# Second attention: 32-row rotary products and two full score passes in place of three, query rotary rows by DRAM

## The chip, the core and the metric

The kernel runs on one core of a Trainium2 chip. Five engines work side by side, each through its own instructions in order: TensorE (PE) multiplies matrices and writes to PSUM, VectorE (DVE) and ScalarE (ACT) do element work and read PSUM, GpSimd (POOL) does element work in SBUF, and SyncE (SP) issues DMA transfers. Instructions of different engines wait for each other by semaphores. The metric is the device time of one execution in microseconds (us); less is better.

## What is computed

A trunk of two layers over 1024 positions of width 1024. The first layer mixes positions by dilated window attention, the second by latent attention with 16 heads, which is where the change is. Cut to that mixer:

```python
def rope(x, cos, sin):
    x1, x2 = x[..., :half], x[..., half:]
    return jnp.concatenate([x1 * cos - x2 * sin, x2 * cos + x1 * sin], axis=-1)

def mixer_mla(u, w_in, q_norm, w_uq, kv_norm, w_ukv, w_out):
    cq, ckv, k_rope, gate = jnp.split(u @ w_in, ...)
    q = (rmsnorm(cq, q_norm) @ w_uq).reshape(B, S, 16, 64 + 32)
    q_nope, q_rope = q[..., :64], q[..., 64:]
    kv = (rmsnorm(ckv, kv_norm) @ w_ukv).reshape(B, S, 16, 64 + 64)
    k_nope, v = kv[..., :64], kv[..., 64:]
    q_rope, k_rope = rope(q_rope, ...), rope(k_rope, ...)
    # for each block of 128 queries, all 16 heads:
    s = (q_nope @ k_nope.T + q_rope @ k_rope.T) * 96 ** -0.5
    o = softmax(s) @ v
    return (o * silu(gate)) @ w_out
```

A head's score is a product over 96 rows: 64 of its own (nope) and 32 rotary ones. The rotary key rows are the same for all heads.

## The kernel before, in words

Every float32 operand of a product is split in two parts, high and low (`h` and `l`): high is the value rounded to the matmul's type, low what is left. `mm3` (lines 89 to 94) makes three PE passes of it: high by high, low by high, high by low. The profile names these passes L92, L93 and L94 wherever they stand; they are told apart by the tile they write.

The second attention is `layer_b_attention`. Its work is 128 **units**: 16 heads by 8 blocks of 128 queries, with all 1024 keys at once. One loop emits it with a lag between its parts, and PE and SP keep the order in which the loop writes their instructions; ACT, DVE and POOL are ordered by the scheduler at build time, and in that order they run. For unit u:

- `front(u)`: scores into the PSUM tile `s` (128 queries by 1024 keys, two banks; two such buffers), three passes for each half of the keys.
- `soft(u)`: DVE takes the row maximum of `s`, negated, into `mb` (L1328).
- `expo(u)`: ACT writes the exponential into `pr` and its row sums into `den` (L1336).
- `middle(u)`: two iterations later, eight PE transposes of `pr` into two PSUM tiles `t` (L1368), cast by ACT to `pth` (L1371), the rest split off by DVE to `ptl` (L1372).
- `back(w)`: for two units at once, 16 PE passes of 256 columns that multiply by the values `vq` into the tile `o` (L1388); for every second w a transpose of the denominators (L1391). ACT copies `o` out as `osum` (L1397, L1398; the denominators as `rden`, L1349), POOL adds its halves and multiplies by the gate (L1399, L1400).

The tiles `t`, `o` and the products of the preparation share four PSUM banks.

Preparation runs inside the loop as generators, one step per call of `next`: `b_qk(p)` makes the q and k rows of the two heads of pair p (9 passes for each half of the positions), `b_turn(p)` the rotary rows of the queries of four heads (12 passes, products with the cosine and sine table on DVE, sums on POOL), `b_v` the values of four heads. A tile of q or k (128 rows) holds the 64 nope rows above and, below, 64 rows for the rotary part, 32 of them filled and the others zero, so that two neighbouring heads share the rotary query rows and differ in where the key rows stand. `b_rope_rows` copies the key rows from tile to tile by DMA of POOL's queue (L1219). `latents_t` puts the rotary key rows into the first two `kb` tiles.

## Time and profile before

| what | value |
|---|---|
| median of 3 runs | 1365.49 us (1363.44 to 1368.98) |
| the profiled execution | 1372.24 us |
| its span, first to last instruction | 1370.4 us |
| mean granted TensorE clock | 0.987 |
| first and last score pass of the second attention start at | 791.2 and 1259.3 us |
| DMA, mean of the span | 83 GB/s |

The span goes from the profile's first instruction to its last; the 1.8 us beside it belong to the execution and to no engine. A busy time is the sum of the time in which an engine had an instruction under way. On PE instructions overlap (a pass of 512 columns lasts 0.39 us and the next starts 0.23 us after it), so distances between starts say what a pass costs. In a row of instructions, the bracket at the end gives the idle time of the engine just before it and the instruction that ended it. A group's row gives its count, then busy time, mean duration in ns, and idle time before it.

### The profile page before, as it was taken

The numbers are of one execution on the slowest core, as the hardware profiler recorded it, in microseconds if no ns is written. First come the engines' busy times: TensorE is split into PE (matmuls) and PEld (weight loads), VectorE is DVE, ScalarE is ACT, GpSimd is POOL, SyncE is SP. The second block draws the span as 40 slices with busy tenths as digits, with TensorE's granted clock in tenths as the row PEclk, the third lists the DMA queues.
The fourth block names the chain that finished last, engine by engine and source line by source line (L and its number), as shares of the span: only waits on it lengthen the run. The fifth ranks groups of instructions, "written<-read, shape, count | busy, mean of one in ns | idle before, by whom it ended". The sixth has DMA issues, their size and how long they took to land.

```text
span 1370.4 us, 20504 instructions
## 1 busy us (share of the span) xinstructions
PE 1339.2 (98%) x7464; PEld 1152.6 (84%) x7464; DVE 855.7 (62%) x1473; ACT 798.4 (58%) x1631; POOL 562.5 (41%) x550
## 2 busy tenths in 40 slices
PE   8999999999999999999999999999999999999997
PEld 7788888888888888888988888898889889898776
DVE  5554454445445344566734278887887887777887
ACT  3575555554443432355742288788788878887421
POOL 0142233123222266614632344744553473444761
PEclk6999999999999999999999999999999999999998
DMA  9422221113244254552154011111112111113322
GB/s 361 109 66 37 60 62 40 37 48 99 85 143 152 64 158 136 186 175 115 62 143 153 0 34 30 24 41 25 30 27 54 30 24 28 25 55 118 114 93 92
DMA packets 44980, 114.28 MB, mean 83 GB/s; under 512 B 6917, under 2 KB 13333, under 8 KB 44880
## 3 DMA queue, kind: packets, MB, share of 16 engines
q1 hardware_dynamic: 40184, 100.43, 24.0%
q0 software_dynamic: 4096, 12.24, 3.6%
q8 instruction: 59, 0.97, 0.3%
q14 instruction: 41, 0.34, 0.1%
q10 hardware_dynamic: 600, 0.32, 0.1%
HBM read 96.42 MB, written 8.67 MB: 77 GB/s over the span
## 4 chain that ended last, share of the span: by engine, by line
PE 73%; DVE 10%; ACT 7%; DMA 5%; issue 4%; SPq 0%; POOL 0%; DVEq 0%; ACTq 0%; POOLq 0%
PE pj L92 8%; PE pj L94 8%; PE pj L93 8%; PE o L1388 6%; PE t L1368 5%; PE s L92 3%; PE s L94 3%; PE s L93 3%; DMA ada<-ada_row 3%; PE ip L265 3%; PE po L92 2%; PE po L94 2%; PE po L93 2%; DVE mb L1328 2%; PE t L564 2%
## 5 line engine op out<-in xcount | busy, mean ns | idle before, releaser
L92 PE MATMUL pj<-uh,wh 128*128 128x512 f32 x528 | 217.5, 412 | 0.0
L94 PE MATMUL pj<-uh,wl 128*128 128x512 f32 x528 | 207.5, 393 | 0.0
L93 PE MATMUL pj<-ul,wh 128*128 128x512 f32 x528 | 207.3, 393 | 0.0
L1328 DVE TENSOR_REDUCE mb<-s 128x1 f32<-128x1024 f32 x128 | 155.6, 1216 | 48.8 <-PE s L94 47.9
L1372 DVE TENSOR_TENSOR ptl<-t,pth 128x512 fp32r<-128x512 f32 x256 | 165.0, 680 | 5.3 <-ACT pth L1371 3.2
L1371 ACT CAST pth<-t 128x512 fp32r<-128x512 f32 x256 | 139.4, 589 | 37.8 <-PE t L1368 34.4
L105 POOL TENSOR_TENSOR wl<-wraw,wh 128x1024 fp32r<-128x1024 f32 x42 | 106.2, 2533 | 123.0 <-ACT wh L104 93.2
L1336 ACT ACTIVATE pr<-s,mb 128x1024 f32<-128x1024 f32 x128 | 144.2, 1126 | 15.1 <-DVE mb L1328 14.5
L1368 PEld LDWEIGHTS t<-ident,pr 128*128 128x128 f32 x1024 | 119.3, 141 | 19.0 <-DVE ptl L1372 2.8
L1368 PE MATMUL t<-ident,pr 128*128 128x128 f32 x1024 | 133.0, 272 | 2.1 <-DVE ptl L1372 2.1
L1388 PE MATMUL o<-pth,vq 128*128 128x256 f32 x512 | 130.4, 292 | 1.1 <-DVE ptl L1372 1.1
L1388 PE MATMUL o<-ptl,vq 128*128 128x256 f32 x512 | 125.5, 283 | 2.0 <-DVE ptl L1372 1.8
L553 ACT ACTIVATE sb<-sb,stat 128x256 f32<-128x256 f32 (+1 forms) x144 | 67.0, 466 | 95.2 <-DVE stat L547 95.1
L94 PEld LDWEIGHTS pj<-uh,wl 128*128 128x128 f32 x528 | 99.4, 188 | 22.3
L1399 POOL TENSOR_TENSOR osum<-osum 64x256 f32<-64x256 f32 x64 | 47.7, 746 | 163.5 <-ACT osum L1398 162.3
L93 PEld LDWEIGHTS pj<-ul,wh 128*128 128x128 f32 x528 | 100.1, 190 | 14.0
L92 PEld LDWEIGHTS pj<-uh,wh 128*128 128x128 f32 x528 | 99.9, 189 | 14.2
L92 PE MATMUL s<-kb,q 128*128 128x512 f32 x256 | 105.8, 413 | 0.1
L94 PE MATMUL s<-kb,q 128*128 128x512 f32 x256 | 100.4, 392 | 0.0
L93 PE MATMUL s<-kb,q 128*128 128x512 f32 x256 | 100.4, 392 | 0.0
L1388 PEld LDWEIGHTS o<-ptl,vq 128*128 128x128 f32 x512 | 97.8, 191 | 3.0 <-DVE ptl L1372 3.0
L1388 PEld LDWEIGHTS o<-pth,vq 128*128 128x128 f32 x512 | 97.5, 191 | 1.7 <-DVE ptl L1372 1.6
(289 smaller groups left out, 3151.2 us busy)
## 6 DMA issues: line engine op xcount, KB each, us to landing
wraw<-wa SPq DMA_DIRECT2D x36, 512.0 KB
ada<-ada_row SPq DMA_DIRECT2D x64, 256.0 KB
wraw<-wo_a SPq DMA_DIRECT2D x18, 512.0 KB
ada<-ada_ss SPq DMA_DIRECT2D x16, 512.0 KB
kb<-kb POOLq DMA_DIRECT2D x30, 256.0 KB, 4.6
f<-f_d SPq DMA_DIRECT2D x18, 256.0 KB
xc<-xt SPq DMA_DIRECT2D x8, 512.0 KB
xr<-x SPq DMA_DIRECT2D x8, 512.0 KB
```

The lines of the kernel that those rows point to most:

```text
L92: mm(out, wh, xh, start=start, stop=False)
L93: mm(out, wh, xl, start=False, stop=False)
L94: mm(out, wl, xh, start=False, stop=stop)
L105: (lo_engine or self.nc.gpsimd).tensor_tensor(l[:, :width], raw[:, :width], f32(h[:, :width]), op=ALU.subtract)
L553: nc.scalar.activation(sb[:, a * w : a * w + w], sb[:, a * w : a * w + w], AF.Exp, bias=stat[:, 0, hh, t : t + 1], scale=-1.0, accum_out=s ...
L1328: nc.vector.tensor_reduce(m[:, 0:1], s, axis=AX.X, op=ALU.max, negate=True)
L1336: nc.scalar.activation(pr, s, AF.Exp, bias=m[:, 0:1], accum_out=dens[u // 8][:, u % 8 : u % 8 + 1])
L1368: nc.tensor.transpose(pt[:, c * P : c * P + P], pr[:, kt * P : kt * P + P], self.ident)
L1371: nc.scalar.copy(h, src)
L1372: nc.vector.tensor_tensor(l, src, f32(h), op=ALU.subtract)
L1388: nc.tensor.matmul(po[:, 0:256], v, pts[j][x][:, c * 256 : c * 256 + 256], start=n == 0, stop=n == 15)
L1399: nc.gpsimd.tensor_tensor(w3[mine, 0:256], w3[mine, 256:512], w3[mine, 0:256], op=ALU.add)
```

## The change

The rotary key rows go into one tile `kr`, whose four strips of 32 rows hold high parts of the two halves of the keys, twice. The lower 64 rows of the q and k tiles now hold what the second and third pass needed, so that two full passes cover the nope rows' three terms and the rotary rows' low terms: `qa` with the high nope rows above and their low part below, against `k[0]` with the high key rows twice; `qb` with the high nope rows and the rotary rows, against `k[1]` with the low key rows and the rotary key terms. The remaining term, high rotary by high rotary, is four products of 32 rows (`tile_position` 0, 32, 64 and 96) that serve two units: strips 0 and 1 the two key halves of the first unit, strips 2 and 3 of the second. `front` therefore makes two units at once and claims both `s` buffers, and the loop goes in steps of two units.

The query's rotary rows are added in place on POOL, split on ACT and POOL, written to DRAM by SP and read back by SP into the lower half of `qb` and into the strips of a tile `q3`. For all pairs but the first, the second copy of the q and k rows is made by SP's DMA instead of a second ACT copy. The key rows for all later heads are copied once before the loop.

```diff
@@ layer_b_in @@
+        self.kr = self.M.tile([P, 512], F32R, name="kr")
-        nc.gpsimd.memset(latn, 0.0)
-            for c in (400, 448):
-                nc.vector.tensor_tensor(t[:, c : c + 16], tmp[:, 0:16], tmp[:, 32:48], op=ALU.subtract)
-                nc.vector.tensor_tensor(t[:, c + 32 : c + 48], tmp[:, 16:32], tmp[:, 48:64], op=ALU.add)
+            rot = t[:, 384:512].rearrange("p (g a c) -> p g a c", g=4, a=2)
+            x = [tmp[:, 16 * n : 16 * n + 16].unsqueeze(1).to_broadcast([P, 4, 16]) for n in range(4)]
+            nc.vector.tensor_tensor(rot[:, :, 0, :], x[0], x[2], op=ALU.subtract)
+            nc.vector.tensor_tensor(rot[:, :, 1, :], x[1], x[3], op=ALU.add)
...
-            for e, (h, l) in enumerate(self.kb):
-                dst.append((h[64:128, c : c + P], l[64:128, c : c + P], slice(64 - 64 * e, 128 - 64 * e), 3))
...
+            for rows in ((slice(0, P),) if i < 4 else (slice(32, 64), slice(96, 128))):
+                nc.scalar.copy(self.kr[rows, sl], pt[rows, 3 * P : 4 * P])
+            nc.vector.tensor_tensor(
+                self.kb[0][1][64:96, c : c + P], pt[32:64, 3 * P : 4 * P], f32(self.kr[32:64, sl]), op=ALU.subtract
+            )
@@ b_rope_rows: once, before the loop @@
-        for src, dst in zip(self.kb[(hd - 2) % 3], self.kb[hd % 3]):
-            self.nc.gpsimd.dma_start(dst[64:128, :], src[64:128, :])
+        for j in range(2):
+            dma(first[96:128, j * 512 : j * 512 + 512], self.kr[32 * j : 32 * j + 32, :])
+        for n in (1, 2):
+            dma(self.kb[n][1][64:128, :], first[64:128, :])
@@ b_turn @@
-                nc.gpsimd.tensor_tensor(dst, ab[row : row + 32, 0:512], ab[row : row + 32, 512:1024], op=op)
-            self.rope[p].append(r0)
+            for rows, op in ((slice(0, 64), ALU.subtract), (slice(64, 128), ALU.add)):
+                nc.gpsimd.tensor_tensor(ab[rows, 0:512], ab[rows, 0:512], ab[rows, 512:1024], op=op)
+            hl = self.ht(F32R, "rope")
+            nc.scalar.activation(hl[:, 0:512], ab[:, 0:512], AF.Copy)
+            nc.gpsimd.tensor_tensor(hl[:, 512:1024], ab[:, 0:512], f32(hl[:, 0:512]), op=ALU.subtract)
+            for a in range(2):
+                for x in range(2):
+                    nc.sync.dma_start(rd[:, x, a, :, sl], f32(hl[64 * a : 64 * a + 64, x * 512 : x * 512 + 512]))
@@ b_qk @@
-        def put(dst, sl, src):
...
-        def rope(hf, part):
...
+            nc.sync.dma_start(f32(qb[64:128, :]), rows.rearrange("x a c t -> (x a c) t"))
+            q3 = third[:, e * 512 : e * 512 + 512]
+            for g in range(4):
+                src = rows[0].rearrange("a c (i z t) -> (a c) i z t", z=2, t=P)[:, :, g // 2, :]
+                nc.sync.dma_start(f32(q3[32 * g : 32 * g + 32, :]).rearrange("p (i t) -> p i t", t=P), src)
...
+        def both(dst, twin, sl, src, rows):
+            nc.scalar.copy(dst[0:64, sl], src)
+            if p:
+                nc.sync.dma_start(f32(twin[rows, sl]), f32(dst[0:64, sl]))
+            else:
+                nc.scalar.copy(twin[rows, sl], src)
...
@@ front @@
-            s = self.PB.tile([P, 1024], F32, tag="s", bufs=2, name=self.nm("s"))
-            ts = slice(t * P, t * P + P)
-            for j in range(2):
-                ks = slice(j * 512, j * 512 + 512)
-                self.mm3(s[:, ks], q[0][:, ts], q[1][:, ts], k[0][:, ks], k[1][:, ks], True, True)
+            s = [self.PB.tile([P, 1024], F32, tag="s", bufs=2, name=self.nm("s")) for _ in range(2)]
+            for g in range(4):
+                rows = slice(32 * g, 32 * g + 32)
+                ks = slice((g % 2) * 512, (g % 2) * 512 + 512)
+                mm(
+                    s[g // 2][:, ks], q3[rows, (t // 2) * P : (t // 2) * P + P], self.kr[rows, :],
+                    start=True, stop=False, tile_position=(32 * g, 0),
+                )
+            for a in range(2):
+                ts = slice((t + a) * P, (t + a) * P + P)
+                for n, (q, kk) in enumerate(((qa, k[0]), (qb, k[1]))):
+                    for j in range(2):
+                        ks = slice(j * 512, j * 512 + 512)
+                        mm(s[a][:, ks], q[:, ts], kk[:, ks], start=False, stop=n == 1)
+                st[u + a] = s[a]
@@ the loop @@
-        for u in range(nu + 4):
-            p, r = u // 16, u % 16
-            if u < nu:
-                front(u)
...
+        for u0 in range(0, nu + 4, 2):
+            if u0 < nu:
+                front(u0)
...
+                soft(u0)
+                soft(u0 + 1)
+            for u in (u0, u0 + 1):
...
+                if 0 <= u - 2 < nu:
+                    middle(u - 2)
...
+                if u < nu:
+                    expo(u)
+                if u == u0 and u >= 4:
...
+                    back((u - 4) // 2)
...
```

What that does to the engines' orders, at three places. PE in the middle of the attention, before: the scores of one unit (`s_8101`) follow a value product, then come the transposes of an older unit and the scores of the next (`s_8128`).

```order
L1391 MATMUL o_8074<-ident,den_7782 4x128
L92 MATMUL s_8101<-kb_5416,q_7074 128x512
L93 MATMUL s_8101<-kb_5417,q_7074 128x512
L94 MATMUL s_8101<-kb_5416,q_7075 128x512
L92 MATMUL s_8101<-kb_5416,q_7074 128x512
L93 MATMUL s_8101<-kb_5417,q_7074 128x512
L94 MATMUL s_8101<-kb_5416,q_7075 128x512
L1368 MATMUL t_8110<-ident,pr_8043 128x128 x4
L1368 MATMUL t_8117<-ident,pr_8043 128x128 x4
L92 MATMUL s_8128<-kb_5418,q_7807 128x512
```

And with the change (the line numbers are the changed file's: L1335 the 32-row products, L1344 the full passes, L1392 the transposes, L1412 the value product), where the names `s_8064` and `s_8065` are the two buffers:

```order
L1335 MATMUL s_8064<-kr,q_1045_7076 128x512 x2
L1335 MATMUL s_8065<-kr,q_1045_7076 128x512 x2
L1344 MATMUL s_8064<-kb_5416,q_7084 128x512 x2
L1344 MATMUL s_8064<-kb_5417,q_7085 128x512 x2
L1344 MATMUL s_8065<-kb_5416,q_7084 128x512 x2
L1344 MATMUL s_8065<-kb_5417,q_7085 128x512 x2
L1392 MATMUL t_8086<-ident,pr_8024 128x128 x4
L1392 MATMUL t_8093<-ident,pr_8024 128x128 x4
L1412 MATMUL o_8102<-pth_8006,vq_6745 128x256
```

Both units' scores now stand together; the sixteen value passes and the transposes of the second unit (`t_8129`, `t_8136`) follow, and then the next four 32-row products, into the same two buffers.

ACT at such a place before: casts of transposes (L1371), an exponential (L1336), the two copies of the value product (L1397, L1398), casts, and the next exponential.

```order
L1371 CAST pth_8137<-t_8141 128x4x128
L1371 CAST pth_8139<-t_8148 128x4x128
L1336 ACTIVATE pr_8156,den_8155<-s_8128,mb_8135 128x1024
L1397 COPY osum_8175<-o_8158 64x256
L1398 COPY osum_8175<-o_8158 64x256
L1371 CAST pth_8137<-t_8197 128x4x128
L1371 CAST pth_8139<-t_8204 128x4x128
L1336 ACTIVATE pr_8211,den_8155<-s_8180,mb_8187 128x1024
```

With the change (L1395 casts, L1360 exponentials, L1373, L1421 and L1422 the copies of the value product):

```order
L1395 CAST pth_8082<-t_8086 128x4x128
L1360 ACTIVATE pr_8100,den_7803<-s_8064,mb_8078 128x1024
L1395 CAST pth_8084<-t_8093 128x4x128
L1373 COPY rden_8120<-o_8102 4x128
L1421 COPY osum_8124<-o_8102 64x256
L1422 COPY osum_8124<-o_8102 64x256
L1360 ACTIVATE pr_8143,den_7803<-s_8065,mb_8080 128x1024
L1395 CAST pth_8082<-t_8129 128x4x128
L1395 CAST pth_8084<-t_8136 128x4x128
```

The second unit's exponential (of `s_8065`) stands behind the copies of the value product, as before, and now ahead of the last two casts.

Behind a `b_turn` ACT has, with the change, the copy of the turned rows (L1260) ahead of the second exponential, and POOL makes those rows (L1258) around an addition of `osum` (L1423). ACT:

```order
L1360 ACTIVATE pr_7635,den_7431<-s_7594,mb_7613 128x1024
L1395 CAST pth_7619<-t_7628 128x4x128
L1421 COPY osum_7654<-o_7637 64x256
L1422 COPY osum_7654<-o_7637 64x256
L1395 CAST pth_7617<-t_7668 128x4x128
L1395 CAST pth_7619<-t_7675 128x4x128
L1260 ACTIVATE rope_7661<-ab_7608 128x512
L1360 ACTIVATE pr_7682,den_7431<-s_7595,mb_7615 128x1024
```

POOL:

```order
L1261 TENSOR_TENSOR rope_7580<-ab_7573,rope_7580 128x512
L1258 TENSOR_TENSOR ab_7608<-ab_7608 64x512
L1423 TENSOR_TENSOR osum_7654<-osum_7654 64x256
L1258 TENSOR_TENSOR ab_7608<-ab_7608 64x512
L1424 TENSOR_TENSOR gT_6151<-osum_7654,gT_6151 64x256
L1261 TENSOR_TENSOR rope_7661<-ab_7608,rope_7661 128x512
```

Before, ACT read the turned rows only in `b_qk`, pairs of units later.

138 lines of the change are left out of this document (62 added, 76 removed).

## The prediction

> **What bounds the kernel now.** I read the page's busy shares first, then the table of stages, the waits of the stage that changes, and its instructions in order of time on three engines.
>
> ```profile
> PE 1339.2 (98%) x7464; PEld 1152.6 (84%) x7464; DVE 855.7 (62%) x1473; ACT 798.4 (58%) x1631; POOL 562.5 (41%) x550
> ```
>
> ```profile
> 900.00:950.00 50.00, 49.54 (x338) 44.67 (x337) 38.00 (x53) 42.76 (x86) 21.34 (x25) 1.00 0.18 39
> ```
>
> ```profile
> PE m L92 <- DVE kb L1298: 3.2, 7, 0.5
> PE t L1368 <- DVE ptl L1372: 2.1, 3, 0.7
> PE o L1388 <- DVE ptl L1372: 1.1, 2, 0.6
> ```
>
> PE is busy 98% of the span. The second line is one stretch of the second attention (busy time of PE, weight loads, DVE, ACT, POOL): PE 49.54 of 50 us, and ACT already 42.76. The last three are all that PE waited for from 800 to 1270 us: 6.4 us. The attention is bound by the number of PE passes, but ACT stands close behind.
>
> ```profile
> L92 PE MATMUL s<-kb,q x256: 389/395/504, 791.2 to 1258.9; 128*128 128x512 f32 x128
> ```
>
> So the stage is the 468 us from the first score pass to the last. Two consecutive pairs of units on PE:
>
> ```profile
> 899.56 0.48 PE L92 MATMUL s<-kb,q 128*128 128x512 f32 x1
> ...
> 901.82 0.36 PE L1388 MATMUL o<-pth,vq 128*128 128x256 f32 x1
> ...
> 903.83 0.48 PE L92 MATMUL s<-kb,q 128*128 128x512 f32 x1
> 904.15 0.40 PE L93 MATMUL s<-kb,q 128*128 128x512 f32 x1
> 904.38 0.39 PE L94 MATMUL s<-kb,q 128*128 128x512 f32 x1
> ...
> 905.31 1.03 PE L1368 MATMUL t<-ident,pr 128*128 128x128 f32 x8
> 906.10 0.48 PE L92 MATMUL s<-kb,q 128*128 128x512 f32 x1
> ...
> 908.35 0.36 PE L1388 MATMUL o<-pth,vq 128*128 128x256 f32 x1
> ...
> 910.34 0.40 PE L92 MATMUL s<-kb,q 128*128 128x512 f32 x1
> ...
> 912.52 0.48 PE L92 MATMUL s<-kb,q 128*128 128x512 f32 x1
> ```
>
> Durations overlap, so I use distances between starts. A score pass costs 0.23 us (904.15 to 904.38), the first of a run 0.32. Six take 1.48 (903.83 to 905.31), eight transposes 0.79 (905.31 to 906.10), the value product 1.99 (908.35 to 910.34). A pair of units costs (912.52 - 899.56)/2 = **6.48 us**, with no gap.
>
> **The change part by part.** *Removed passes.* Twelve score passes of a pair become eight plus a group of four 32-row products. Eight take 1.48 + 2 x 0.23 = 1.94. No row shows 32-row products. If the four run together the group costs one pass, 0.23; if one after the other, 0.92. I take 0.45: one pass, plus twice the 0.09 by which a first pass exceeds the others, rounded up. PE's work in a pair is then 0.45 + 1.94 + 2 x 0.79 + 1.99 = 5.96, against 6.48: 0.52 less, 33 us over 64 pairs, if PE stays the bound.
>
> A rule of the Trainium skill (TensorEngine Tiling (Array Packing), Key Properties) speaks against it: a change of the tiling mode drains the array. The rows would price a drain at a pass's duration less its spacing, 0.39 - 0.23 = 0.16, and two a pair make 0.32, so that the group costs 0.55 and 64 pairs lose 6 us of the 33; no run so far shows it.
>
> *The new wait.* Before, the two `s` buffers alternate: a unit's scores wait only for the exponential of two units ago. Now both are claimed at once, and the third 32-row product cannot start until the previous pair's second exponential has read its buffer. Behind it on PE stand all eight passes. ACT works in order and has that exponential behind the two copies of the value product (the order above), which wait for PE. So it is a loop. On ACT and DVE:
>
> ```profile
> 904.11 0.26 ACT L1349 COPY rden<-o 4x128 f32<-4x128 f32 x1 [0.27 <-PE o L1391]
> 904.39 0.36 ACT L1397 COPY osum<-o 64x256 f32<-64x256 f32 x1
> 904.77 0.37 ACT L1398 COPY osum<-o 64x256 f32<-64x256 f32 x1
> 905.94 1.08 ACT L1371 CAST pth<-t 128x512 fp32r<-128x512 f32 x2 [0.81 <-PE t L1368]
> 906.90 1.13 ACT L1336 ACTIVATE pr<-s,mb 128x1024 f32<-128x1024 f32 x1
> 907.91 0.21 ACT L1336 ACTIVATION_READ_ACCUMULATOR pr<-s,mb 128x1 f32 x1
> 908.20 1.07 ACT L1371 CAST pth<-t 128x512 fp32r<-128x512 f32 x2
> ...
> 910.54 0.36 ACT L1397 COPY osum<-o 64x256 f32<-64x256 f32 x1 [0.17 <-PE o L1388]
> ```
>
> ```profile
> 905.51 1.23 DVE L1328 TENSOR_REDUCE mb<-s 128x1 f32<-128x1024 f32 x1 [1.79 <-PE s L94]
> 906.65 1.28 DVE L1372 TENSOR_TENSOR ptl<-t,pth 128x512 fp32r<-128x512 f32 x2
> ```
>
> From the end of one second exponential to the end of the next: hand-over and the two released products 0.45 (bounds 0.23 and 0.92), eight passes 1.94, transposes 0.79, from the value product's start to its first copy 2.19 (908.35 to 910.54), or 2.57 in every second pair with its denominators (901.82 to 904.39), mean 2.38, two copies 0.76, exponential 1.13. The sum is **7.45 us**, longer than PE's 5.96 and longer than the 6.48 of today. Nothing else is later: the first cast comes 0.63 after the transposes start (905.31 to 905.94), at 3.02; the first exponential 0.48 later at 3.5, the second cast 1.30 later (906.90 to 908.20) at 4.8, done in time for the copy at 5.37 at the earliest. DVE must first finish the two splits of the previous transposes: the casts start 0.16 after the loop's start (1.30 less 1.13) and follow 0.48 apart, each split needs 0.6 behind its cast, so the first maximum starts near 2.0; two maxima at 1.14 end by 4.4.
>
> By the order of the change 29 pairs are plain: 29 x (7.45 - 6.48) = **+28**.
>
> *Pairs with preparation products behind the value product* (14 with nine passes, 3 with twelve, 3 with 24 half passes). PE's work there is at least 5.96 + 9 x 0.23 = 8.0, above the loop, so they gain the 0.52: 20 x 0.5 = **-10**.
>
> *Pairs right behind these.* ACT's casts of the new q and k rows stand ahead of its exponentials.
>
> ```profile
> L1270 ACT CAST q<-m 64x512 fp32r<-64x512 f32 x28 | 16.3, 582 | 5.4 <-DVE q L1271 5.2
> L1244 DVE TENSOR_TENSOR ab<-m,cs 64x512 f32<-64x512 f32 x12 | 8.2, 687 | 5.7 <-PE m L94 3.7 <-issue 1.8
> L1279 POOL TENSOR_TENSOR q<-rope,q 64x512 fp32r<-64x512 f32 x16 | 20.3, 1291 | 3.1 <-ACT q L1277 2.8
> L1399 POOL TENSOR_TENSOR osum<-osum 64x256 f32<-64x256 f32 x63 | 46.7, 741 | 163.4 <-ACT osum L1398 162.3
> ```
>
> Behind a `b_qk` or a `b_v` four casts of 0.58, two of 0.48 and a weight split (taken as one more of 0.58) come before or beside the first exponential: 3.9 less the 0.5 that ran ahead, then 1.30, two casts 0.96, two copies 0.76 and 1.13 make 7.6: 10 pairs x 1.1 = **+11**. Behind a `b_turn` the second exponential stands behind a copy that waits for POOL: maxima until 4.6, four DVE products of 0.69 until 7.4, POOL's subtraction 1.29, an `osum` addition 0.74, POOL's addition 1.29, the copy 0.6 and the exponential 1.13 end at 12.4, 5.9 more than now: 3 x 6 = **+18** (bounds 0, if POOL is early, and 18).
>
> *The last pair of heads* has ACT splits of the output weights in four pairs of units, two with the next casts too, ahead of the second exponential:
>
> ```profile
> L104 ACT ACTIVATE wh<-woraw 128x1024 fp32r<-128x1024 f32 x6 | 6.4, 1064 | 1.1 <-DMA woraw<-wo_b 1.1
> ```
>
> 4 x 1.06 and 2 x 0.96: **+6**. Against all this, the stage of today holds some waits of its own: 64 x 6.48 = 415, 162 preparation passes at 0.23 = 37 and 96 half passes at 0.12 (1.99 / 16) = 12 make 464, less 5 for the first pairs, which lack transposes and value product. The 468 hold some 9 more, about half of it first passes of a run at 0.09 and half waits, which the periods above replace: **-5**.
>
> *At nothing:* the rotary rows by DRAM, and the q and k copies now sent by SP. They are issued some 20 us before the head that reads them; the nearest row:
>
> ```profile
> kb<-kb POOLq DMA_DIRECT2D x26, 256.0 KB, 4.6
> ```
>
> 4.6 us to landing. Without that cover each of seven changes of heads would pay up to 4.6, 32 us. On SP only the denominator's two small transfers queue behind them, and those are read five units later. The first pair alone has no such lead: its rows are written and read back while 10 us of gate passes remain: **+2**. The fewer key copies before the attention lie beside a full PE: 0. Fewer ACT casts and POOL subtractions in `b_qk` are in the periods above.
>
> Sum: 28 - 10 + 11 + 18 + 6 - 5 + 2 = **+50 us**. The profiled execution took 1372.2 (span 1370.4 and 1.8 around it), so 1422; it lay 6.7 above the median of 1365.5, where I forecast **1415**.
>
> **The rivals.** *PE stays the bound (the other side).* The 0.52 of every pair is kept: 1365.5 - 33 = **1332**. It decides at 5.96: the second exponential would have to end by then instead of at 7.45. It would, just, if it stood ahead of the copies: first exponential at 3.5, the next 1.30 later, 4.8 + 1.13 = 5.9. ACT's 42.76 busy us in 50 speak for a tight but possible fit; the built order speaks against, in every pair. The Trainium skill (TensorE: Matmul & The Clock Gate, Part 3) gives 3.07 times for four such products; by it the group takes 0.92/3.07 = 0.30, an estimate, and this rival 1322. 5%.
>
> *Only the loop bites.* POOL and the casts are on time and the last pair is no worse: 28 - 10 + 2 = +20, **1386**. For it: preparation overlaps well today. 20%.
>
> *The four products don't run together.* The change then doesn't do what it says: the group costs 0.92, the 20 preparation pairs gain 0.05 and not 0.5, and the loop grows by up to 0.47 in 42 pairs: +50 + 9 + 20 = **1444**. Nothing in this trace speaks for or against. 15%.
>
> **How the numbers follow.** The forecast itself has 57%. The remaining 3% are small offsetting errors that end within 0.5% (about 7 us, what a measurement of this kernel can tell from no change). The range takes in the loop alone at its low end and the serial case at the other: 1384 to 1445, which leaves out the 8% of the other cases. Faster 0.05, same 0.03, slower 0.92.
>
> **What would show it.** PE's share of a plain stretch falls from 99% to about 80%, and a wait of the 32-row products for ACT's exponential, which is absent now, totals 60 to 90 us in some 40 occasions; ACT's copy of `osum` still starts right behind PE. The group shows in four starts within 0.1 us of each other or 0.23 apart. Behind a `b_turn` ACT waits for POOL three times. I am wrong if the distance between groups is near 6 us in plain pairs, or if PE waits for DMA instead.

## The result, and the profile after

| | before | after |
|---|---|---|
| median of 4 runs | 1365.55 us (1363.44 to 1368.98) | **1454.91 us** (1447.96 to 1455.41) |
| ratio, with its 95% interval | | **1.0645** (1.0617 to 1.0673) |
| the profiled execution's span | 1370.4 us | 1453.0 us |
| mean granted TensorE clock | 0.987 | 0.977 |

The change costs 89 us. The forecast was 1415 with a range up to 1445: the direction was right, the size was not. The page of the changed kernel gives the busy time and share of each engine first:

```profile
PE 1361.3 (94%) x7464; PEld 1138.8 (78%) x7464; DVE 863.6 (59%) x1449; ACT 783.6 (54%) x1611; POOL 491.7 (34%) x483
```

The same stretch of the second attention as before (length; busy time and instructions of PE, weight loads, DVE, ACT, POOL; clock; DMA):

```profile
900.00:950.00 50.00, 45.54 (x303) 37.86 (x302) 35.45 (x48) 36.42 (x75) 13.49 (x16) 1.00 0.25 63
```

PE is busy 45.5 of 50 us where it was 49.5, though the change was to save it work. ACT and DVE have become idler too: 36.4 for 42.8 and 35.5 for 38.0. Every engine is idler and the time is longer, which points to engines that wait for each other in a ring. The waits of PE from 790 to 1345 us (engine, line and product, releaser; sum, times, longest):

```profile
PE s L1335 <- ACT pr L1360: 45.8, 43, 2.6
PE t L1392 <- ACT osum L1422: 7.8, 4, 2.4
PE s L1335 <- DMA q<-rope_d: 6.7, 1, 6.7
PE o L1412 <- DVE kb L1314: 5.6, 6, 0.9
PE m L92 <- DVE vq L1221: 3.7, 3, 1.2
```

The first line is the wait that the prediction named. The other four are new as well, and the prediction had none of them as a wait of PE; the third is a wait for DMA, which it had named as a sign of being wrong. A plain pair on PE and ACT, in order of time (start, length, engine, line, operation; idle time before it and what ended it):

```profile
862.99 0.49 PE L1335 MATMUL s<-kr,q 32*128 32x512 f32 x2
...
864.52 0.49 PE L1335 MATMUL s<-kr,q 32*128 32x512 f32 x2 [1.04 <-ACT pr L1360]
864.94 2.12 PE L1344 MATMUL s<-kb,q 128*128 128x512 f32 x8
...
866.90 1.03 PE L1392 MATMUL t<-ident,pr 128*128 128x128 f32 x8
...
870.64 0.49 PE L1335 MATMUL s<-kr,q 32*128 32x512 f32 x2
...
871.96 0.49 PE L1335 MATMUL s<-kr,q 32*128 32x512 f32 x2 [0.82 <-ACT pr L1360]
872.38 2.11 PE L1344 MATMUL s<-kb,q 128*128 128x512 f32 x8
```

```profile
863.26 1.11 ACT L1360 ACTIVATE pr<-s,mb 128x1024 f32<-128x1024 f32 x1
...
869.93 0.36 ACT L1421 COPY osum<-o 64x256 f32<-64x256 f32 x1 [0.23 <-PE o L1412]
870.31 0.37 ACT L1422 COPY osum<-o 64x256 f32<-64x256 f32 x1
870.70 1.11 ACT L1360 ACTIVATE pr<-s,mb 128x1024 f32<-128x1024 f32 x1
```

The ring can be walked through. The second exponential ends at 863.26 + 1.11 = 864.37, the second two 32-row products start at 864.52, the full passes at 864.94, the transposes at 866.90, the copy of the value product on ACT at 869.93, the next second exponential at 870.70, and it ends at 871.81: 7.44 us a turn. This turn has no denominators; the prediction's 7.45 is a mean of turns with and without them, and its sum without them is 7.26. The first two 32-row products (862.99, 870.64) are early and help nothing, since the full passes stand behind the other two. They also hide a part of the wait: it goes from 862.99 to 864.52, 1.53 us, but the profile counts only the 1.04 behind their own 0.49 as idle.

**Where the 82.6 us of the two spans are.** One fixed point lets the parts be compared: the activation that ends the sixth block of gate products, shortly before the rotary rows of the first heads are made.

```profile
762.81 0.60 ACT L1120 ACTIVATE gT<-pg 128x512 f32<-128x512 f32 x1 [4.84 <-PE pg L94]
...
791.17 0.39 PE L92 MATMUL s<-kb,q 128*128 128x512 f32 x1
```

```profile
759.99 0.60 ACT L1127 ACTIVATE gT<-pg 128x512 f32<-128x512 f32 x1 [4.84 <-PE pg L94]
...
787.11 0.47 PE L92 MATMUL m<-lath,wuh 128*128 128x512 f32 x1 [2.37 <-DVE kb L1314]
...
798.18 2.07 PE L1335 MATMUL s<-kr,q 32*128 32x512 f32 x4 [6.73 <-DMA q<-rope_d]
```

The first fence is before, the second after. On SP the trip through DRAM of the same rows looks like this, eight writes and then the first read:

```profile
778.58 8.07 SPq L1264 DMA_DIRECT2D rope_d<-rope  x8
794.48 0.50 SPq L1281 DMA_DIRECT2D q<-rope_d  x1
```

Up to that point the changed kernel was 2.8 ahead; from there to the first full pass (800.19) it takes 40.2 us where 28.4 stood: **+11.8**. The 63 distances between the first full passes of neighbouring pairs of units (before the change: between the first score passes) add up to 536.8 where they were 462.6: **+74.1**. The rest of the span is 0.6 shorter. So the part behind the fixed point went from 607.6 to 693.0, +85.4. By kinds of pairs (mean distance, and what the kind adds in all; the predicted terms by the same kinds):

| pairs | before | after | adds | predicted |
|---|---|---|---|---|
| 18 plain | 6.50 | 7.61 | +20.0 | +17.5 |
| 14 with nine preparation passes, 3 with `b_turn` | 8.92, 9.37 | 8.31, 9.02 | -9.6 | -8.5 |
| 3 with `b_v` | 9.61 | 10.61 | +3.0 | -1.5 |
| 7 behind `b_qk`, 3 behind `b_v` | 6.35, 6.36 | 8.57, 7.32 | +18.4 | +11 |
| 3 behind `b_turn` | 7.37 | 12.21 | +14.5 | +18 |
| 3 behind those | 6.93 | 9.51 | +7.7 | +2.9 |
| 6 of the last heads | 6.76 | 8.89 | +12.8 | +11.8 |
| first 3 | 5.61 | 8.03 | +7.2 | +1.9 |

The predicted column spreads the +28 of the 29 plain pairs over the plain ones (18), those behind the ones behind `b_turn` (3), the last heads (6) and the first (2). It leaves out the prediction's -5 for stalls of before, and the start's +2 against 11.8. With these the prediction had +50 behind the fixed point.

### The profile page after: what moved, and what is told of

Read it like the earlier page. It is cut to its first block, busy times and chain, and to the rows that moved or that the text cites. A ratio compares the mean times of both kernels' runs of the same rounds, so it can differ in the third digit from the quotient of the medians.

```text
span 1453.0 us, 20632 instructions
## 1 busy us (share of the span) xinstructions
PE 1361.3 (94%) x7464; PEld 1138.8 (78%) x7464; DVE 863.6 (59%) x1449; ACT 783.6 (54%) x1611; POOL 491.7 (34%) x483
## 5 line engine op out<-in xcount | busy, mean ns | idle before, releaser
L1395 ACT CAST pth<-t 128x512 fp32r<-128x512 f32 x256 | 140.6, 587 | 96.5 <-PE t L1392 96.2
L1352 DVE TENSOR_REDUCE mb<-s 128x1 f32<-128x1024 f32 x128 | 152.6, 1220 | 30.2 <-PE s L1344 29.4
L1360 ACT ACTIVATE pr<-s,mb 128x1024 f32<-128x1024 f32 x128 | 142.8, 1115 | 35.5 <-DVE mb L1352 34.7
L1344 PE MATMUL s<-kb,q 128*128 128x512 f32 x512 | 144.7, 427 | 0.0
L1392 PE MATMUL t<-ident,pr 128*128 128x128 f32 x1024 | 136.8, 277 | 7.9 <-ACT osum L1422 7.8
L1423 POOL TENSOR_TENSOR osum<-osum 64x256 f32<-64x256 f32 x64 | 47.3, 739 | 279.5 <-ACT osum L1422 276.4
L1392 PEld LDWEIGHTS t<-ident,pr 128*128 128x128 f32 x1024 | 120.0, 143 | 22.4 <-ACT osum L1422 10.1
L1412 PE MATMUL o<-pth,vq 128*128 128x256 f32 x512 | 130.5, 293 | 6.3 <-DVE kb L1314 5.6
L1412 PE MATMUL o<-ptl,vq 128*128 128x256 f32 x512 | 125.1, 282 | 0.0
L1344 PEld LDWEIGHTS s<-kb,q 128*128 128x128 f32 x512 | 97.3, 200 | 34.9 <-issue 16.3
L1335 PE MATMUL s<-kr,q 32*128 32x512 f32 x256 | 56.3, 508 | 52.6 <-ACT pr L1360 45.8
L1412 PEld LDWEIGHTS o<-pth,vq 128*128 128x128 f32 x512 | 97.8, 191 | 8.0 <-ACT pr L1360 6.8
L1412 PEld LDWEIGHTS o<-ptl,vq 128*128 128x128 f32 x512 | 98.0, 191 | 0.0
```

The lines of the kernel that those rows point to most:

```text
L1344: mm(s[a][:, ks], q[:, ts], kk[:, ks], start=False, stop=n == 1)
L1352: nc.vector.tensor_reduce(m[:, 0:1], s, axis=AX.X, op=ALU.max, negate=True)
L1360: nc.scalar.activation(pr, s, AF.Exp, bias=m[:, 0:1], accum_out=dens[u // 8][:, u % 8 : u % 8 + 1])
L1392: nc.tensor.transpose(pt[:, c * P : c * P + P], pr[:, kt * P : kt * P + P], self.ident)
L1395: nc.scalar.copy(h, src)
L1412: nc.tensor.matmul(po[:, 0:256], v, pts[j][x][:, c * 256 : c * 256 + 256], start=n == 0, stop=n == 15)
```

## The experiments

Each edit is made to the changed kernel. "The part behind the fixed point" is the span less the start of that activation, 693.0 in the changed kernel; it is given because the changed kernel and all these edits are the same up to there, and yet their profiled executions reach it at times from 753.7 to 762.7 us. Differences of a few us between medians can come from there.

### Both exponentials ahead of the copies

```diff
+                if u == u0 and u < nu:
+                    expo(u0)
+                    expo(u0 + 1)
-                if u < nu:
-                    expo(u)
                 if u == u0 and u >= 4:
```

> The changed kernel (1454.9 us) with one thing moved: both exponentials of a pair of units are written ahead of the value product, so that on ACT the second one stands ahead of the copies of the value product. Theory 1 (a loop through ACT: second exponential, 32-row products, eight passes, value product, its copies, second exponential): the loop loses the value product and the two copies and becomes hand-over 0.57, passes 1.94, first cast at +0.63 and 0.48 long, exponential with its sum 1.29, cast 0.48, exponential 1.13: 6.5 us in a plain pair where it is 7.44 and 7.77 now. 29 plain pairs give back 30 us, the three pairs behind a b_turn 5 us each, the pairs behind a b_qk some: 1400 to 1420 in all. Rival (the 32-row products and the switch of the array's tiling are what costs): nothing of that is moved here, plain pairs stay at 7.4 to 7.8 and the time at 1450 to 1456.

Measured: **1394.26 us** (1392.67 to 1397.40), ratio 1.0207 (1.0176 to 1.0238); behind the fixed point 635.6, 57.4 less. PE's waits from 790 to 1285 us:

```profile
PE o L1412 <- DVE kb L1314: 5.5, 6, 0.9
PE t L1392 <- DVE ptl L1396: 5.3, 6, 1.3
PE s L1335 <- DMA q<-rope_d: 5.1, 1, 5.1
PE s L1335 <- ACT pr L1360: 3.1, 3, 1.5
```

The 45.8 us of waits for the exponential have shrunk to 3.1, with two lines of the loop moved and no work taken away. Plain pairs fall from 7.61 to 6.51 in the mean. The ring through the copies is shown to be the main cause, and it is worth somewhat more than expected. But 6.51 is just the 6.50 of before: what PE's passes save in a pair does not come back even here.

### One unit's scores first

Two 32-row products and four full passes for the first unit, then the same for the second.

```diff
-            for g in range(4):
-                mm(s[g // 2][:, ks], ..., tile_position=(32 * g, 0))
             for a in range(2):
+                for g in (2 * a, 2 * a + 1):
+                    mm(s[a][:, ks], ..., tile_position=(32 * g, 0))
                 ts = slice((t + a) * P, (t + a) * P + P)
```

> The changed kernel with the four 32-row products in two groups: two of them and the four full passes of the first unit, then two and the four passes of the second, so that the first unit's passes no longer stand behind the wait for the second buffer. Theory 1 (the loop): four passes of 0.23 leave the loop; plain pairs go from 7.6 to about 6.7, 29 of them give back 26 us; the 20 pairs with preparation, bound by PE, pay one more start of a group, about 0.5 each, 10 us: 1432 to 1445. Rival (the switch of the tiling is what costs): twice the switches, at 0.3 to 0.5 us each in 64 pairs, 1475 to 1485.

Measured: **1415.53 us** (1414.89 to 1416.91), ratio 1.0361 (1.0332 to 1.0390); behind the fixed point 658.1. This is the other way to cut the same ring: four full passes no longer stand behind the second exponential. It takes away 34.9 us where at most 23 were expected, with plain pairs at 6.75 to 6.88 and those behind a `b_qk` at 7.4 to 7.6. The mode of the array is changed twice as often here, and the time falls, against the rival's 1475 to 1485.

### DVE's half split left out, alone and with the exponentials ahead

```diff
+                if j == 0:
-                nc.vector.tensor_tensor(l, src, f32(h), op=ALU.subtract)
+                    nc.vector.tensor_tensor(l, src, f32(h), op=ALU.subtract)
...
-                        nc.tensor.matmul(po[:, 0:256], v, pts[j][x][:, ...
+                        nc.tensor.matmul(po[:, 0:256], v, pts[j][x * (1 - j)][:, ...
```

> The change with DVE's split left out for the second half of the keys and nothing else. Theory 1 (the loop of the change runs over PE, ACT's copies and ACT's exponential, and DVE is no part of it): plain pairs stay at 7.4 to 7.8 and the total at 1450 to 1456. Rival (DVE's work is part of what sets the pairs already): plain pairs fall by 0.3 or more, total below 1445.

> Both exponentials ahead of the copies, and DVE's split left out for the second half of the keys (the value product uses the high part twice there, so PE has the same passes): 1.3 us less of DVE in a pair. Theory 1 (with the exponential ahead, plain pairs stand at 6.4 to 6.65 instead of PE's own 6.05 because DVE's two maxima and four splits run one behind the other): plain pairs fall to 6.05 to 6.25, total 1378 to 1386. Rival (ACT's casts, exponentials and copies set them): plain pairs stay within 0.1, total 1391 to 1397.

Measured, alone: **1454.47 us** (1453.14 to 1456.48), ratio 1.0643 (1.0620 to 1.0666), plain pairs 7.4 to 7.8 as without the edit. Taking 1.3 us of splits from DVE in every pair changes nothing, so they are no part of the change's ring. With the exponentials ahead: **1387.19** (1386.53 to 1389.35), ratio 1.0154 (1.0128 to 1.0180), between the two expectations. Pairs of 6.65 and 6.63 fall to 6.28 and 6.35, those of 6.39 stay at 6.45. So DVE's order is part of what keeps the plain pairs above PE's own work. How much PE's own work is, this kernel shows: the first pair here has no wait, and in the second the third and fourth 32-row products come late.

```profile
909.43 2.12 PE L1344 MATMUL s<-kb,q 128*128 128x512 f32 x8
...
915.28 0.50 PE L1335 MATMUL s<-kr,q 32*128 32x512 f32 x4
915.71 2.12 PE L1344 MATMUL s<-kb,q 128*128 128x512 f32 x8
...
921.41 0.81 PE L1335 MATMUL s<-kr,q 32*128 32x512 f32 x4
922.15 2.12 PE L1344 MATMUL s<-kb,q 128*128 128x512 f32 x8
```

915.71 - 909.43 = 6.28 with denominators; without them the pairs behind a `b_v`, which have no wait, take 6.14. So PE's own pair is 6.14 and not the predicted 5.96. Before, the same pairs took 6.54 and 6.37, so the change saves PE 0.2 to 0.3 us in a pair and not 0.52. The second distance is 6.44, because the four products take 0.81 where they take 0.50: a wait of 0.31 for the second buffer that the profile does not count as idle. The waits for the exponential that it does count, 8.3 us now for 3.1, lie outside the plain pairs.

### The group twice

The same loop over the four 32-row products is written a second time, with `start=False`.

> The four 32-row products are issued twice in a row, so the rotary term is counted twice. Theory 1 (the four run together; most of the group's 0.53 us is the change of array mode): the second group costs one pass, 0.23 us, or at most the whole 0.43 again; it lies on the loop or on PE in all 64 pairs, so +15 to +27 us on 1454.9: 1470 to 1482. Rival (the four run one after the other, and 0.53 is only what the trace happens to show): 0.92 us in 64 pairs, +59: about 1514.

Measured: **1469.20 us** (1466.89 to 1471.79), ratio 1.0732 (1.0714 to 1.0751), just under the 1470 to 1482 of theory 1. A plain pair on PE, where L1342 is the second group:

```profile
937.95 0.50 PE L1335 MATMUL s<-kr,q 32*128 32x512 f32 x2 [1.05 <-ACT pr L1367]
937.96 0.73 PE L1342 MATMUL s<-kr,q 32*128 32x512 f32 x4
938.62 2.11 PE L1351 MATMUL s<-kb,q 128*128 128x512 f32 x8
```

Plain pairs become 7.67 where they were 7.44: **0.23 us** for four more products, which is one pass. The four run together, and the rival of 1444 by serial products is out. In the changed kernel, where nothing waits, the group costs this:

```profile
919.49 0.40 PE L94 MATMUL m<-lath,wul 128*128 128x512 f32 x1
...
919.82 0.50 PE L1335 MATMUL s<-kr,q 32*128 32x512 f32 x4
...
920.25 2.10 PE L1344 MATMUL s<-kb,q 128*128 128x512 f32 x8
```

From the last product ahead of it to the first full pass it is 0.76, less that product's own 0.23: 0.53. Less the four products' 0.23, some 0.30 are left for going into the 32-row mode and out of it; behind transposes it is some 0.07 more. The Trainium skill (TensorEngine Tiling (Array Packing), Key Properties) states a drain at a change of mode without a price. These rows would be its price, but they don't show the drain itself; the 0.55 that the prediction worked out for it and did not take is close.

### The turned rows put off

ACT's copy of the turned rotary rows, POOL's split and their DRAM writes come two steps (for the second half four) behind the end of `b_turn`.

```diff
-            hl = self.ht(F32R, "rope")
-            nc.scalar.activation(hl[:, 0:512], ab[:, 0:512], AF.Copy)
...
+            late.append((sl, ab))
+        for sl, ab in late:
+            yield 0.0
+            yield 0.0
+            finish(sl, ab)
```

> The changed kernel with the ACT copy, POOL split and DRAM writes of the turned rotary rows put off by about one pair of units, for all heads but the first four. Theory 2 (the pair behind a b_turn is 12.2 us long because the second exponential stands behind a copy that waits for POOL, and the pair behind that one is 9.1 to 9.95 us long because PE stood idle so long that its clock was halved): the first goes to 8 or 9, the second to 7.5, three times, and the granted clock has no halved stretch there: 1454.9 - 3 x (4 + 2) = 1437, 1432 to 1442. Rival (these pairs are long for PSUM banks held by the products of b_turn): the long pair stays near 12 and the time within 3 us of 1455.

Measured: **1452.69 us** (1450.79 to 1457.26), ratio 1.0635 (1.0593 to 1.0677); behind the fixed point 692.8 against 693.0. The pair behind `b_turn` falls from 12.26 to 9.88, but the next two, 9.95 and 8.25, become 9.75 and 9.83: four pairs together take 37.9 for 38.9 there, and 37.9 for 38.3 and 37.8 for 37.9 at the other two places. The wait of the transposes for ACT's copy turned into one for DVE's split (7.1 us in 3 times). So neither side is right: the long pair did fall, as theory 2 said, but the time moved to the next pairs, and the total is the rival's.

### Idle time filled

Dummy products in the places where PE stands still behind `b_turn`, into parts of PSUM that are overwritten or unused.

```diff
+            if w in (8, 24, 40):
+                for _ in range(40):
+                    nc.tensor.matmul(po[:, 384:512], v, pts[1][1][:, 0:P], start=True, stop=True)
...
+            if u in (22, 54, 86):
+                for _ in range(12):
+                    mm(s[0][:, 0:512], qa[:, 0:P], k[0][:, 0:512], start=True, stop=True)
```

> The changed kernel with products added in the three pairs behind a b_turn only: 40 of 128 columns into an unused part of the value product's bank, and 12 score passes into the first score buffer ahead of the next pair, where they are overwritten. They fill most of the time in which PE waits there. Theory of the clock: PE's idle time is what halves the granted clock for 7 to 10 us; filled, the halved stretches at these three places go, the pair that follows falls from 9.1 to 9.95 to about 7.5, and the time falls by 3 to 8 us in spite of the added work: 1447 to 1452. Rival (the following pair is long for another reason, such as DVE behind its schedule): it stays above 9, and the added passes make the time equal or longer, 1455 to 1462.

The rows that led to it, in the changed kernel behind a `b_turn`, and the clock in the stretches around them (second to last numbers: clock, DMA share, GB/s):

```profile
888.67 1.97 PE L1392 MATMUL t<-ident,pr 128*128 128x128 f32 x8 [2.38 <-ACT osum L1422]
...
892.94 0.80 PE L1335 MATMUL s<-kr,q 32*128 32x512 f32 x2 [1.58 <-ACT pr L1360]
893.66 3.78 PE L1344 MATMUL s<-kb,q 128*128 128x512 f32 x8
```

```profile
885.00:890.00 5.00, 2.62 (x17) 2.42 (x17) 4.45 (x7) 3.11 (x7) 4.10 (x5) 0.84 0.13 34
890.00:895.00 5.00, 3.42 (x11) 1.95 (x10) 1.38 (x2) 2.62 (x5) 2.95 (x3) 0.50 0.25 79
895.00:900.00 5.00, 5.00 (x25) 4.31 (x25) 3.49 (x4) 2.38 (x4) 0.00 (x0) 0.64 0.25 65
```

Behind an idle time of 2.38 us the clock stands at one half for about 10 us, and eight full passes last 3.78 instead of 2.12. With the idle time filled, the clock is full from 813.1 to 1260.2 us (this execution is some 6 us earlier, so the stretches hold slightly later work):

```profile
885.00:890.00 5.00, 5.00 (x26) 3.71 (x25) 1.67 (x3) 2.77 (x6) 2.69 (x3) 1.00 0.26 82
890.00:895.00 5.00, 4.69 (x38) 4.06 (x36) 3.26 (x4) 3.70 (x8) 0.47 (x1) 1.00 0.25 82
```

The pairs behind fall from 9.95, 9.53 and 9.06 to 7.65, 7.66 and 7.66: 5.6 us, of the +7.7 in that row of the table. The filled pairs ahead of them are 1.1 longer each, 3.4 in all, which gives the other engines more time too; but the eight full passes alone, at 3.78, 3.78 and 3.52 instead of 2.12, are 4.7 of the 5.6. So most of that row is the clock. The median is **1447.12** (1445.73 to 1448.96), ratio 1.0592 (1.0561 to 1.0622), inside the expectation; but behind the fixed point it is 692.4 for 693.0, and the profiled execution reached that point 6.2 earlier. The median's gain is therefore no evidence; the pairs and the clock are.

### The first heads' rotary rows earlier

Four kernels: `b_turn(0)`, which makes these rows, made whole ahead of the last gate products; the same with the exponentials ahead and the turned rows put off; `b_turn(0)` two blocks of gate products earlier; and that with the exponentials ahead. The first one's edit:

```diff
-        weave((chain(gate(6, 1, ...), gate(7, 1, ...)), 10368.0), (chain(self.b_turn(0), self.b_qk(0)), 9000.0))
+        for _ in self.b_turn(0):
+            pass
+        weave((chain(gate(6, 1, ...), gate(7, 1, ...)), 10368.0), (self.b_qk(0), 9000.0))
```

> The rotary query rows of the first four heads are made wholly ahead of the last gate products instead of between them, so that their trip through DRAM starts about 2 us earlier on PE's side, and 15 more gate passes (3.4 us) stand between it and the first score pass. Theory 1 (PE's wait of 6.7 us before the first scores is the trip through DRAM): the wait falls to 2 to 4 us, the first full pass starts at 794 to 797 instead of 800.2, and the total falls by 3 to 6: 1449 to 1452. Rival (ACT's and DVE's casts of the first q and k rows are nearly as late): the first full pass at 799 or later, total within 2 us of 1455.

> Three edits together: both exponentials ahead of the copies (1394 alone), the turned rows' copy, split and DRAM writes put off for all but the first four heads, and the first four heads' rows made ahead of the gate products. Theory 1 (with PE near its own bound the put-off rows find room, and the start gains by itself): pairs behind b_turn fall from 8.4 to 9.0 to about 7.5, start -3 to -5: 1384 to 1389. Rival (as when put off alone, the time only moves to the next pairs): pairs 11 and 12 together stay near 16 us, and only the start gains: 1389 to 1393. Neither reaches 1366, because plain pairs stay at 6.4 to 6.6 behind DVE's maxima and splits.

> The rotary query rows of the first four heads are made two blocks of gate products earlier than in the change (some 78 gate passes, 18 us, before the last product they need), so that neither their sums on POOL nor their trip through DRAM is late. From the first product of the preparation to the first full pass the change takes 28.8 us where 17.0 stood before; the passes alone are 17.1. Theory 1 (the waits of 2.4 and 6.7 us and the halved clock behind them are the whole difference): PE waits less than 2 us in all there, and the total falls by 8 to 11: 1444 to 1447. Rival (the casts of the first q and k rows on ACT and DVE are late by themselves): PE still waits 4 us or more for DVE's key split, total 1450 to 1455.

> Both exponentials ahead of the copies (1394.3 alone) and the first four heads' rotary rows two blocks of gate products earlier. If the two losses are separate, the gains add: 1383 to 1387. Rival (the loop hides a late start, since the first pairs then wait for less): 1390 to 1394. Either way above 1367, since the pairs behind the preparation and the plain ones keep their times.

The first: **1455.23** (1449.00 to 1458.75), ratio 1.0625 (1.0595 to 1.0654). PE's wait for the DMA is gone, and PE waits for DVE instead; the first full pass comes 1.4 earlier behind the fixed point, and the first three pairs take 2.3 more:

```profile
789.16 0.77 PE L92 MATMUL m<-lath,wuh 128*128 128x512 f32 x1 [5.32 <-DVE kb L1316]
...
794.86 0.48 PE L92 MATMUL pg<-u1h,wgh 128*128 128x512 f32 x1 [1.66 <-DVE kb L1316]
```

ACT's casts of the first k rows, which that split needs, stand behind ACT's copy of the turned rows, which waits for POOL's sums. The second: **1399.61** (1396.69 to 1404.63), ratio 1.0222 (1.0189 to 1.0254), 4.7 longer behind the fixed point than with the exponentials ahead alone: neither theory, since the pairs behind `b_turn` did not become shorter, those with preparation behind the put-off work became longer (8.22 to 8.62 or 9.24, 9.27 to 9.74 twice), and the start gained only 0.6. The third: **1445.33** (1441.52 to 1453.95), ratio 1.0584 (1.0539 to 1.0629), where 1444 to 1447 was expected; but only 7.0 of it lie behind the fixed point (0.8 ahead of the first full pass, 3.3 in the first three pairs, which ran at full clock, the rest later), and PE still waits, now ahead of other gate products for their weights, with half the clock from 764.3 to 774.6:

```profile
766.40 0.79 PE L92 MATMUL pg<-u1h,wgh 128*128 128x512 f32 x1 [4.56 <-ACT wgh L1170]
...
769.11 0.80 PE L94 MATMUL pg<-u1h,wgl 128*128 128x512 f32 x1 [1.49 <-POOL wgl L1171]
```

The fourth: **1394.75** (1392.15 to 1395.74), ratio 1.0202 (1.0179 to 1.0225), no gain over the exponentials ahead, nearest the rival. So the trip through DRAM is what ends last at the start, but ACT's copy and POOL's sums of the turned rows are nearly as late, and moving them moves the wait. A version without the loss of the start was not found.

### The splits of q, k and v from SBUF

First the key rows alone, then all three; the low parts become zero.

```diff
-                nc.vector.tensor_tensor(k[1][0:64, sl], ps[...], f32(k[0][0:64, sl]), op=ALU.subtract)
+                src = ps[64 * e : 64 * e + 64, :] if p < 2 else f32(k[0][0:64, sl])
+                nc.vector.tensor_tensor(k[1][0:64, sl], src, f32(k[0][0:64, sl]), op=ALU.subtract)
```

> For pairs of heads 2 to 7, DVE's split of the key rows reads the rounded rows in SBUF instead of the product in PSUM (the low part becomes zero), so the product's PSUM bank comes free at ACT's copy; the instruction stays. Theory 1 (the value product waits for that bank): the six pairs behind such a b_qk fall from 8.6 to about 7.7 us, and PE's wait of the value product for DVE's key split goes: 1455 - 6 = about 1449. Rival (the casts of q and k on ACT ahead of the exponentials set those pairs, as predicted with 7.6 but longer): they stay at 8.4 to 8.7, total within 3 us of 1455.

> For pairs of heads 2 to 7 and the values of heads 4 to 15, DVE's splits of the new q, k and value rows read the rounded rows in SBUF (the low parts become zero), so every PSUM bank of a preparation product comes free at ACT's copy. The splits stay as instructions. Theory 1 (banks held until DVE's splits lengthen the pairs behind b_qk and the pairs with b_v): pairs behind b_qk of pairs 2 to 7 fall from 8.57 to about 7.7, the pairs with b_v from 10.6 to about 9.4: 6 x 0.9 + 3 x 1.2 = 9 less, about 1446. Rival (ACT's casts ahead of the exponentials set both kinds): they stay within 0.2, total 1452 to 1457.

> The same with both exponentials ahead of the copies (1394.3 alone). Theory 1 (banks): behind b_qk 7.53 falls to about 6.7, with b_v 10.5 to 9.4, total about 1386. Rival (casts on ACT): within 0.2 of the pairs before, total 1391 to 1397.

The row behind a `b_qk` that led to it, in the changed kernel: the value product waits for a bank of PSUM, not for its data.

```profile
924.16 0.36 PE L1412 MATMUL o<-pth,vq 128*128 128x256 f32 x1 [0.94 <-DVE kb L1314]
```

With the key rows alone: **1458.02** (1454.52 to 1469.28), ratio 1.0664 (1.0618 to 1.0711). That wait fell to 1.0 in all, and a new one took its place, of the transposes for the query rows' split: 7.0 in 5 times. The six pairs did not fall as theory 1 said; they took 7.9 to 9.9, and DVE's key splits themselves became longer (rows below). So this kernel does not tell the two theories apart. With all three: **1446.69** (1442.02 to 1447.71), ratio 1.0578 (1.0549 to 1.0607), behind the fixed point 683.9, 9.1 less. Five of the six pairs concerned fall from 8.6 to 7.4 or 7.5, the sixth from 8.26 to 8.01, and the pairs with `b_v` from 10.61 to 9.89, while two of the three behind these rose from 7.3 to 7.8. The same pair in that kernel, from its first full pass to the next one's:

```profile
920.70 2.12 PE L1344 MATMUL s<-kb,q 128*128 128x512 f32 x8
...
928.16 2.12 PE L1344 MATMUL s<-kb,q 128*128 128x512 f32 x8
```

928.16 - 920.70 = 7.46, a plain turn of the ring. A faster DVE is not the reason. These are its key splits from 860 to 1290 us in the changed kernel, with the key rows alone, and with all three (mean ns is the second number behind the bar):

```profile
L1314 DVE TENSOR_TENSOR kb<-m,kb 64x512 fp32r<-64x512 f32 x24 | 16.5, 686 | 0.4
L1314 DVE TENSOR_TENSOR kb<-kb 64x512 fp32r<-64x512 f32 x24 | 22.4, 955 | 0.3
L1314 DVE TENSOR_TENSOR kb<-kb 64x512 fp32r<-64x512 f32 x24 | 19.0, 802 | 0.2
```

Reading SBUF, the splits last as long or longer (the queries' 683 for 689, the values' 873 for 686). The scheduler orders ACT's and DVE's work here a little differently too, but the time is that of the bank: in the changed kernel the value product starts 3.91 behind the first full pass, right after DVE's key splits end at 924.02, and with all three it starts 2.75 behind it, before those splits begin at 923.71. That is 1.16 of the 1.18 by which this pair falls. So the banks that DVE's splits hold cost these pairs what ACT's casts were predicted to cost. With the exponentials ahead it brings nothing: **1399.52** (1396.80 to 1402.95), ratio 1.0238 (1.0204 to 1.0272), above both expectations. The pairs behind `b_qk` stay at 7.6 to 7.9, and PE waits 15.9 us for DVE's `ptl` splits there. Which order of DVE would serve both was not tried.

## Why the prediction was wrong in size

Of the part behind the fixed point the prediction had +50, and it was +85.4. The mechanism that it named, the ring through the copies, is the largest part of the loss. The 35 us that are missing lie for the most part in three steps of its sum, which stand below under "Wrong". The median missed the forecast by 40 us; what is beyond these 35 lies ahead of the fixed point and in the scatter of the runs.

Right, or nearly so:

- *The new wait.* The ring is as described, and moving the exponentials ahead of the copies takes 57.4 us away. The plain pairs are 7.61 in the mean against 7.45, +2.5 in 18 pairs. The step that was too short is the hand-over, 0.57 from the exponential's end to the full passes instead of 0.45. PE's idle time for it, 45.8 us in 43 times, is less than the 60 to 90 named, and PE's share of the stretch shown fell to 91% and not to 80%. Both miss for one reason: the first two products of a group run during the wait. With their 0.49 in each of 43 times it would be 67 us, an estimate from the rows above.
- *Pairs with preparation*: -0.6 in those with nine passes, against -0.5.
- *Behind a* `b_turn`: 12.2 us against 12.4, by the chain that was worked out. In the first such pair DVE's four products end at 888.21, POOL's two sums with the `osum` addition between them at 891.01, ACT's copy at 891.79 and the second exponential at 892.80.
- *The last pair of heads*: +12.8 against 11.8, in part by luck. The weight splits stand ahead of the second exponential as described, but the clock is at one half from 1301.4 to 1304.8 and from 1311.6 to 1315.0, and eight full passes take 3.33 and 3.56 there instead of 2.11, 2.7 us that the sum didn't have.
- *Own stalls of before: -5.* This is no miss of its own: the table's rows before hold such stalls (7.37 and 6.93 behind `b_turn`, against 6.48).

Wrong, in the order of size:

- *At nothing ... the first pair alone has no such lead: +2.* It was **+11.8** up to the first full pass, and the first three pairs added 7.2 where 1.9 were predicted. The working had the 4.6 us of another transfer as its only price of the trip, and set it against the gate passes that were left. But SP sends its last write at 785.82 and can send the first read only at 794.48, when the writes have landed: 8.7 us for one leg (8.4 and 8.7 in the two kernels with these rows earlier), and then come five reads. Nor did it price the chain ahead (POOL's sums, ACT's copy, POOL's split, eight writes sent one by one), nor that ACT's casts of the first k rows queue behind that copy. It is the step that failed most: a transfer's lead must be counted from the last instruction that feeds it, and for each of its legs.
- *Pairs right behind these: four casts ..., 7.6, +11.* It was **+18.4**. The cause was not ACT's casts but PSUM banks held until DVE's splits; with the splits reading SBUF the pairs behind a `b_qk` took 7.46. The tiles `t`, `o` and the preparation share four banks, and the prediction followed engines only. It is also part of why the pairs with `b_v` became +3.0 instead of -1.5: freed of it, they fell by 0.7 each, some 2.2 in all.
- *No term for the clock.* Between 755 and 1350 us the clock of before was full. After, it stood at one half in seven stretches there, 41 us in all, though PE was idle in part of them. Some 5 us in the pairs behind those behind `b_turn` are shown to come from it. It also lies in the first pairs, which took 3.3 us less in the kernel where they ran at full clock, and in those of the last heads; there it wasn't tested apart.
- *PE's work in a pair*: 6.14 and not 5.96, since the group costs 0.53 to 0.60 and not 0.45. It didn't bear on the forecast, where the ring was longer, but on the rival below.

How the clock follows PE's idle time can't be told from the longest single gap. The Trainium skill (TensorE: Matmul & The Clock Gate, Why this matters for your kernels) warns of idle gaps above some 3 us. Here half the clock followed gaps of 2.38 and 2.42 us, less than that, and in the kernel before it did not follow a gap of 3.04, where the clock stayed at 1.00:

```profile
1316.70 0.47 PE L92 MATMUL po<-wh,ytb 128*128 128x512 f32 x1 [3.04 <-DVE zb L1512]
```

The measurement decides. In the clock records of these traces the changes lie on a fixed grid of 3.41 us. Cut by that grid from 750 to 1400 us, the sixteen traces have 2849 steps at full clock. In 57 of them PE was busy for less than 43% of the step, and half the clock followed every time; in 2673 it was busy for over 65%, and it followed twice; in the 119 between, 52 times. The 3.04 us above lay across two steps of 54% and 57%; the stretch from 884.96 to 888.37, ahead of the row with 2.38, has 39%.

The rivals: *PE stays the bound* named the order that would reach it, the second exponential ahead of the copies, at 5.9 us a pair. That order was built: 6.34 to 6.67. So even the right order leaves this change 2% above before: of the 28.0 us that remain behind the fixed point (635.6 for 607.6) 11.6 are the start, 4.7 the first three pairs, 8.2 those behind `b_qk`, 3.7 those behind `b_turn`, and the plain pairs gain nothing. None of the experiments beat the kernel before.

## What to carry to other kernels

Before two buffers are claimed at once, find the instruction that will release the later one and walk the ring from it back to itself in each engine's order: the sum of the ring, not the sum of PE's work, is the new period, and moving the releasing instruction ahead in that order (57 us here) can be worth more than the passes saved. A ring that idles PE also has to be charged for the clock behind the idle time and for PSUM banks whose release hangs on a queued reader. Compare parts of the program from a point that both versions share, since an earlier part can scatter by more than the effect.

## What the runs showed of the hardware that was not expected

- Four 32-row products in four strips cost one pass together, 0.23 us, and the mode change around them about 0.30.
- Half the clock came behind a step of the 3.41 us grid in which PE was busy for less than 43% (57 of 57), whatever the single gaps: gaps of 2.38 and 2.42 us brought it, one of 3.04 across two steps did not, and neither did those of 0.8 to 1.05 us in every plain pair.
- Rows written to DRAM could be read back only 8.4 to 8.7 us after the last write was sent, in three kernels.
- DVE's splits were no faster from SBUF than from PSUM (the keys' 802 for 686 ns with all three splits changed).
- Up to the fixed point the changed kernel and its fourteen edits are one program, and took from 753.7 to 762.7 us: more than several of the effects looked for.
